# A hybrid decoder trunk: the point in the first layer at which the next layer's constants are loaded

## The chip, the cores and the metric

The kernel runs on one core of a Trainium2 chip. The metric is the device time of one execution in microseconds (us). The kernel before takes 841.26 us, the median of three runs (839.94 to 841.27). Engines are named as in the profile: PE (matmul), PEld (its weight loads), DVE (vector), ACT (scalar, activation functions), POOL, SP. "ACTq" and "SPq" are DMA issues of the ACT and the SP instruction stream.

## The reference

Two layers act on a stream of 256 tokens by 1024 channels. Each layer normalises the stream, projects it with one wide matrix, and feeds three mixers: a Mamba-2 scan (A), sliding-window attention (B) and forgetting attention (C). Their outputs are projected, weighted by gates, merged, projected once more and added to the stream. The lines that matter here:

```python
for layer in range(DEPTH):                       # DEPTH = 2
    h = rms_norm(x, norm_w[layer])
    proj = jnp.einsum('bsd,de->bse', h, w_in[layer])
    ... = jnp.split(proj, split_at, axis=-1)
    y_a = mamba2_branch(a_xbc, a_z, a_dt, conv_w[layer], conv_b[layer], dt_bias[layer],
                        a_log[layer], d_skip[layer], ssm_norm_w[layer])
    y_b = sliding_window_branch(b_q, b_k, b_v, b_z, sinks[layer], cos, sin)
    y_c = forgetting_attention_branch(c_q, c_k, c_v, c_f, c_z, f_bias[layer])
    branch = jnp.einsum('bsiw,iwd->bsid', jnp.stack([y_a, y_b, y_c], axis=2), w_proj[layer])
    g = jax.nn.sigmoid(gates.reshape(b, s, N_BRANCH, d) + gate_bias[layer])
    x = x + jnp.einsum('bsd,de->bse', jnp.sum(g * branch, axis=2), w_out[layer])
return rms_norm(x, final_norm_w)
```

The small parameters among these (`conv_w`, `conv_b`, `ssm_norm_w`, `norm_w`, `dt_bias`, `f_bias`, `sinks`, `a_log`, `d_skip`) are the "constants of a layer".

## The kernel before

**Matmuls.** Every dense product is made of three passes with operands split into a high and a low part: weights arrive from DRAM as 128x1024 float32 pieces (`raw`, six buffers, loaded by SP, line 345). ACT makes `hi` of a piece (L268), DVE makes `lo` = raw - hi (L269), and PE multiplies hi*hi, hi*lo and lo*hi (L97). When DVE has made `lo`, the `raw` buffer is free and SP issues the next load into it. So a late `hi` makes a late `lo`, and this makes a late load, six pieces further on.

**Order of the work.** The kernel writes a list of operations per layer (`op`): queries, keys and values of B, gates of B, the convolutions of A, then keys and queries of C (`u_ck`, `u_cq`, four pairs) with the gate path `z` of C among them, then `gates_proj(0)` (gates and projection of A) and `gates_proj(2)` (of C), then the output projection. Parts that hang on other engines (softmax, the scan) are generators that a "pump" enters between the matmuls. PE runs in the order in which this is written. The other engines are ordered by a scheduler at build time, except for instructions that are pinned to program order. The constants' loads are pinned (`pdma`).

**The constants.** `layer_consts` issues ten DMAs from ACT's instruction stream: `conv_w`, `conv_b` and `ssm_norm_w` into `vr`, `norm_w` into `nwb` (128x1024, broadcast to all partitions, 512 KB), `dt_bias`, `f_bias`, `sinks` and `a_log` into `hb`, and two halves of `d_skip` into `dsk`. POOL then scales `nwb` once. The profile names all of them L263, the line of the pinning helper. Nothing reads the second layer's constants before the end of the first layer. For the last layer the same place in the list holds `load_final`, which loads the weight of the final norm (L1085).

**DMA and semaphores.** Every DMA of SP and ACT counts up one of eight semaphores, DMAHW0 to DMAHW7, given out in rotation over both streams. Before an engine issues a DMA, its instruction stream waits until the DMA that had this semaphore before has landed. While ACT's stream waits so, the activations behind it in the stream wait too.

**Who waits for whom around the forgetting attention.** In the stretch that the change reaches, ACT evicts transposed probabilities from PSUM (L594), computes the `tanh` of a z path (L829) and makes `hi` (L268). DVE finishes z (L832), makes `lo` (L269), multiplies the scan's decays (L804, L805) and adds the scan's result (L815, tile `mx` to `L`). PSUM tiles `mx` rotate through five buffers, so that the last of four score tiles of the next attention quad (`mx<-qt`, L97) can be written only when the first L815 has read the buffer before.

Of the kernel before, what the change touches and what calls it, by code (L numbers as in the profile page):

```python
# [20 lines left out]
L = 2  # L21
# [23 lines left out]
def hybrid_trunk(  # L45
# [17 lines left out]
    def T(tag, shape, dtype=F32, bufs=None):  # L63
        count[0] += 1
        return sb.tile(shape, dtype, tag=tag, name=f"{tag}_{count[0]}",
                       bufs=bufs if bufs is not None else BUFS.get(tag, 1))
# [63 lines left out]
    def pump(budget=BUDGET):  # L130
        t0 = clock["t"]
        while clock["t"] - t0 < budget:
            for m in sorted(waiting, key=lambda m: (m[0], m[1])):
                if ready(m):
                    enter(m)
                    break
            else:
                return
# [119 lines left out]
    def halves(ap):  # L258

        return ap.rearrange("p (a i) -> p a i", a=2)  # L260

    def pin(f):
        return lambda *a, **k: tc.keep_in_program_order(f(*a, **k))  # L263
# [138 lines left out]
    layers = []  # L402
# [9 lines left out]
    def layer_consts(y):  # L412
        l = y.l
        vr = T("vr", [88, P])
        pdma(vr[0:64, :], conv_w[l].rearrange("j (u p) -> (j u) p", p=P))
        pdma(vr[64:80, :], conv_b[l:l + 1, :].rearrange("o (u p) -> (o u) p", p=P))
        pdma(vr[80:88, :], ssm_norm_w[l:l + 1, :].rearrange("o (u p) -> (o u) p", p=P))
        if l:
            y.nwb = T("nwb", [P, D])
            pdma(y.nwb, norm_w[l:l + 1, :].to_broadcast([P, D]))  # L420
            pin(nc.gpsimd.tensor_scalar)(y.nwb, y.nwb, -0.5, None, op0=ALU.mult)
        y.hb = T("hb", [P, 64], bufs=2)
        for i, v in enumerate((dt_bias, f_bias, sinks, a_log)):
            pdma(y.hb[:, 16 * i:16 * i + 16], v[l:l + 1, :].to_broadcast([P, 16]))
        y.dsk = T("dsk", [P, NK], bufs=2)
        for half in range(2):
            src = d_skip[l:l + 1, :].rearrange("o (j two) -> two o j", two=2)[half]
            pdma(y.dsk[64 * half:64 * half + 64, :], src.to_broadcast([64, NK]))
        y.vr = vr
# [14 lines left out]
    def chan(y, w, c):  # L444

        p = pmm()
        dense(p[:, 0:S], lambda k: w.hi(k)[:, c:c + P], lambda k: w.lo(k)[:, c:c + P],
              lambda k: tokens_in_turn(y.hTh, k), lambda k: tokens_in_turn(y.hTl, k), w)
        return ordered(p[:, 0:S])
# [433 lines left out]
    def u_ck(y, j, c):  # L883
        def f(w):
            p = chan(y, w, c)
            y.ckT[j] = T("qt", [P, 2, S])
            act(halves(y.ckT[j][:, 0, :]), p, AF.Copy)
            if j % 2 == 0:
                launch(2, fox_quad(y, j), D_FOX)
            pump()  # L890
        return f

    def u_cq(y, j, c):
        def f(w):
            p = chan(y, w, c)
            kq = y.ckT[j]
            act(halves(kq[:, 1, :]), p, AF.Copy)
            y.cqdone[j] = clock["t"]
            pump()
        return f  # L900
# [187 lines left out]
    def sub(src, n=256):  # L1088
        subs.append((src, n))
        return len(subs) - 1  # L1090

    def op(i, *fs):
        for f in fs:
            ops.append((i, f))

    for y in layers:
        l = y.l
# [3 lines left out]
        def cols(c0, n=256):  # L1101
            return sub([(0, w[:, c0:c0 + n])], n)

        def z1(c0, br, b):
            op(cols(c0 + 256 * b), u_z(y, br, 2 * b, 0), u_z(y, br, 2 * b + 1, P))
# [5 lines left out]
        def gates_proj(br):  # L1111
            def g(b):
                c = 512 * b
                op(cols(C_G + D * br + c, 512), u_gate(y, br, c, 0), u_gate(y, br, c, 1))

            def p(b):
                c = 512 * b
                if b == 0 and br != 0:
                    op(None, lambda y=y: split_late(y, br))
                i = sub([(0, w_proj[l, br, :, c:c + 512])], 512)  # L1120
                if b == 0 and br == 0:
                    op(i, u_proj2(y, br))
                else:
                    op(i, u_proj(y, br, c, 0), u_proj(y, br, c, 1))
            seq = [(g, 0), (p, 0), (g, 1), (p, 1)]
            if br == 0:
                seq = [(lambda b: z1(C_ZA, 0, b), b) for b in range(4)] + seq
            return [lambda f=f, b=b: f(b) for f, b in seq]
# [33 lines left out]
        for b, zb in enumerate(((), (0,), (1,), (2, 3))):  # L1162
            op(cols(C_CK + 256 * b), u_ck(y, 2 * b, 0), u_ck(y, 2 * b + 1, P))
            op(cols(C_CQ + 256 * b), u_cq(y, 2 * b, 0), u_cq(y, 2 * b + 1, P))
            for z in zb:
                z1(C_ZC, 2, z)
        for f in gates_proj(0):
            f()
        op(None, load_final if l + 1 == L else lambda: layer_consts(layers[1]))
        for f in gates_proj(2):  # L1170
            f()
        o = [sub([(0, w_out[l, :, c:c + n])], n) for c, n in ((0, 256), (256, 512), (768, 256))]
# [96 lines left out]
```

## Time and profile before

| what | value |
|---|---|
| median of three runs | 841.26 us (runs of 839.94, 841.26 and 841.27) |
| the profiled execution's own time | 840.8 us |
| its span | 839.1 us, so 1.7 us lie around the span |
| busy: PE, PEld, DVE, ACT, POOL | 824.1, 752.4, 642.5, 502.9, 130.3 us |
| mean granted PE clock | 0.997 |
| DMA | 158.41 MB, mean 189 GB/s |

The profile's page gives busy time by engine, the course of the span in 40 slices, the chain of work that ended last, and groups of instructions. The trace behind it gives each instruction's start, duration, the idle time ahead of it on its engine and what ended this idle time (in brackets, with an arrow). Times in rows are us from the start of the span.

### The profile page before, as it was taken

The numbers are of one execution on the slowest core, as the hardware profiler recorded it, in microseconds if no ns is written. First come the engines' busy times: TensorE is split into PE (matmuls) and PEld (weight loads), VectorE is DVE, ScalarE is ACT, GpSimd is POOL, SyncE is SP. The second block draws the span as 40 slices with busy tenths as digits, with TensorE's granted clock in tenths as the row PEclk, the third lists the DMA queues.
The fourth block names the chain that finished last, engine by engine and source line by source line (L and its number), as shares of the span: only waits on it lengthen the run. The fifth ranks groups of instructions, "written<-read, shape, count | busy, mean of one in ns | idle before, by whom it ended". The sixth has DMA issues, their size and how long they took to land.

```text
span 839.1 us, 15714 instructions
## 1 busy us (share of the span) xinstructions
PE 824.1 (98%) x5832; PEld 752.4 (90%) x5832; DVE 642.5 (77%) x1347; ACT 502.9 (60%) x978; POOL 130.3 (16%) x167
## 2 busy tenths in 40 slices
PE   7999999999999999999999999999999999999996
PEld 7989888989999998887989998898899999988896
DVE  5778987998766679647688889889968667785665
ACT  6466777665656667435555667775456667654442
POOL 7411300000231010210014122000003110121000
PEclk9999999999999999999999999999999999999999
DMA  8576565567475556647677465465756564476632
GB/s 303 164 231 199 178 201 164 176 214 226 140 210 173 157 165 205 206 167 266 205 230 225 151 201 177 144 189 199 240 168 187 161 186 155 150 238 213 214 102 74
DMA packets 123596, 158.41 MB, mean 189 GB/s; under 512 B 12784, under 2 KB 84192, under 8 KB 123520
## 3 DMA queue, kind: packets, MB, share of 16 engines
q1 hardware_dynamic: 109456, 140.79, 53.2%
q10 hardware_dynamic: 14016, 16.49, 6.5%
q8 instruction: 46, 0.75, 0.4%
q14 instruction: 30, 0.25, 0.1%
q0 software_dynamic: 48, 0.13, 0.0%
HBM read 155.22 MB, written 2.16 MB: 188 GB/s over the span
## 4 chain that ended last, share of the span: by engine, by line
PE 91%; DMA 5%; DVE 1%; issue 1%; ACT 1%; POOL 0%; SPq 0%; POOLq 0%; DVEq 0%; ACTq 0%
PE mm L97 79%; PE mx L97 9%; PE mx L101 4%; DMA raw<-in_w_in_dram 3%; DMA raw<-in_w_proj_dram 2%; DVE lo L269 0%; DMA hb<-in_sinks_dram 0%; ACT hi L268 0%; POOL lo L1201 0%; ACT hi L1200 0%; DVE L L474 0%; ACT L L1060 0%; DVE L L269 0%; DVE L L987 0%; DVE L L986 0%
## 5 line engine op out<-in xcount | busy, mean ns | idle before, releaser
L97 PE MATMUL mm<-hi,L 128*128 128x512 f32 (+1 forms) x1344 | 373.8, 364 | 1.9 <-ACT hi L1200 1.3
L269 DVE TENSOR_TENSOR lo<-raw,hi 128x1024 fp32r<-128x1024 f32 x252 | 307.8, 1236 | 88.1 <-ACT hi L268 80.8
L268 ACT ACTIVATE hi<-raw 128x1024 fp32r<-128x1024 f32 x252 | 262.8, 1055 | 94.6 <-PE mm L97 64.8
L97 PE MATMUL mm<-L,hi 128*128 128x256 f32 x1792 | 317.4, 278 | 0.8 <-DVE L L477 0.8
L97 PEld LDWEIGHTS mm<-L,hi 128*128 128x128 f32 x1792 | 277.7, 192 | 7.2 <-issue 3.9
L97 PEld LDWEIGHTS mm<-hi,L 128*128 128x128 f32 x1344 | 241.7, 190 | 32.3 <-issue 2.7
L97 PE MATMUL mm<-L,lo 128*128 128x256 f32 x896 | 246.6, 275 | 0.0
L97 PE MATMUL mm<-lo,L 128*128 128x512 f32 (+1 forms) x672 | 241.7, 361 | 0.1
L97 PEld LDWEIGHTS mm<-L,lo 128*128 128x128 f32 x896 | 172.0, 192 | 0.2
L97 PEld LDWEIGHTS mm<-lo,L 128*128 128x128 f32 x672 | 127.5, 190 | 14.8 <-POOL lo L1201 0.3
L914 POOL TENSOR_SCALAR_AFFINE_SELECT bias<-bias 128x128 f32<-128x128 f32 x64 | 39.8, 653 | 264.0 <-DVE L L793 173.0
L768 DVE SCALAR_TENSOR_TENSOR L<-L,vec,L 128x255 f32<-128x255 f32 (+2 forms) x96 | 46.8, 488 | 6.5 <-ACT L L765 5.1
L97 PE MATMUL mx<-L,L 128*64 128x128 f32 (+1 forms) x384 | 36.5, 332 | 0.0
L97 PEld LDWEIGHTS mx<-L,L 128*64 128x64 f32 x384 | 23.8, 137 | 11.7 <-issue 2.7
L640 ACT ACTIVATE pp<-pp,nm 128x128 f32<-128x128 f32 x64 | 25.1, 394 | 15.0 <-DVE nm L633 11.3
L565 ACT ACTIVATE pp<-pp,nm 128x128 f32<-128x128 f32 x64 | 28.2, 443 | 8.5 <-DVE nm L559 8.5
L938 ACT ACTIVATE L<-L 128x512 f32<-128x512 f32 x24 | 15.1, 629 | 28.6 <-DVE L L937 28.4
L829 ACT ACTIVATE L<-mm 128x256 f32<-128x256 f32 x48 | 18.1, 377 | 19.0 <-PE mm L97 18.9
L771 ACT ACTIVATE L<-L 128x256 f32<-128x256 f32 x32 | 13.3, 417 | 26.3 <-DVE L L768 25.7
L665 POOL TENSOR_SCALAR_AFFINE_SELECT L<-L 128x256 f32<-128x256 f32 x16 | 11.9, 743 | 109.2 <-ACT L L663 109.2
L101 PE MATMUL mx<-ident,L 128*128 128x128 f32 x144 | 22.3, 279 | 3.7 <-DVE L L987 2.1
L633 DVE CUSTOM_DVE_ANT_0 pp<-mx,wmask,nsink 128x128 f32<-128x128 f32 x64 | 24.2, 413 | 2.0 <-PE mx L97 1.8
(176 smaller groups left out, 756.7 us busy)
## 6 DMA issues: line engine op xcount, KB each, us to landing
raw<-in_w_in_dram SPq DMA_DIRECT2D x200, 512.0 KB, 4.6
raw<-in_w_proj_dram SPq DMA_DIRECT2D x48, 512.0 KB, 5.7
raw<-in_w_out_dram SPq DMA_DIRECT2D x16, 512.0 KB, 5.0
L<-cumd ACTq DMA_DIRECT2D x8, 512.0 KB, 4.5
bias<-cumd ACTq DMA_DIRECT2D x16, 256.0 KB, 3.8
L<-in_gate_bias_dram ACTq DMA_DIRECT2D x12, 256.0 KB, 4.0
L<-in_x_dram SPq DMA_DIRECT2D x2, 512.0 KB, 5.0
nwb<-in_norm_w_dram SPq DMA_DIRECT2D x1, 512.0 KB, 5.4
```

The lines of the kernel that those rows point to most:

```text
L97: nc.tensor.matmul(o, a, b, **kw)
L101: nc.tensor.transpose(o, a, i)
L268: keep(act)(hi, src, AF.Copy)
L269: keep(tt)(lo, src, hi.bitcast(F32), op=ALU.subtract)
L565: act(pp[:, i, sl], pp[:, i, sl], AF.Exp, scale=-1.0, bias=nm[:, e:e + 1], accum_out=sums[:, e:e + 1])
L633: nc.vector.tensor_tensor_reduce(out=pp[:, i, sl], in0=score(p, i, b), in1=m, scale=-0.125, scalar=ns[:, i:i + 1], op0=ALU.add, op1=ALU.mi ...
L640: act(pp[:, i, sl], pp[:, i, sl], AF.Exp, scale=-1.0, bias=nm[:, e:e + 1], accum_out=sums[:, e:e + 1])
L768: stt(a[:, s:S], x_[:, 0:S - s], y.vec[:, 16 * j + u:16 * j + u + 1], a[:, s:S], op0=ALU.mult, op1=ALU.add)
L771: act(th, a, AF.Tanh)
L829: act(halves(th), p, AF.Tanh, scale=0.5)
L914: nc.gpsimd.affine_select(out=bias[:, i, dst], in_=bias[:, i, src], compare_op=ALU.is_ge, fill=NEG, base=0, pattern=[[-1, P]], channel_mul ...
L938: act(g, g, AF.Tanh, scale=0.5)
```

## The change

One call moves up in the list of operations. In the first layer it is `layer_consts` of the second layer, in the second layer `load_final`. It stood between the projections of A and the gates of C, and now stands amid the keys and queries of C, behind the second of four pairs.

```diff
         for b, zb in enumerate(((), (0,), (1,), (2, 3))):
             op(cols(C_CK + 256 * b), u_ck(y, 2 * b, 0), u_ck(y, 2 * b + 1, P))
             op(cols(C_CQ + 256 * b), u_cq(y, 2 * b, 0), u_cq(y, 2 * b + 1, P))
+            if b == 1:
+                op(None, load_final if l + 1 == L else lambda: layer_consts(layers[1]))
             for z in zb:
                 z1(C_ZC, 2, z)
         for f in gates_proj(0):
             f()
-        op(None, load_final if l + 1 == L else lambda: layer_consts(layers[1]))
         for f in gates_proj(2):
             f()
```

PE's order of instructions is the same in both kernels, and SP's order of loads too. The load of the last norm's weight stays at its row in ACT's stream, early in the second layer, where the scheduler had put it already. What moves lies in the first layer.

**ACT, at the place that the loads leave** (gates of A and C; `hi` and `raw` are the weight pieces). Before:

```order
L268 ACTIVATE hi_4564<-raw_4465 128x1024
L263 DMA vr_4572<-in_conv_w_dram 64x128
L263 DMA vr_4572<-in_conv_b_dram 16x128
L263 DMA vr_4572<-in_ssm_norm_w_dram 8x128
L263 DMA nwb_4576<-in_norm_w_dram 128x1024
L263 DMA hb_4579<-in_dt_bias_dram 128x16
L263 DMA hb_4579<-in_f_bias_dram 128x16
L263 DMA hb_4579<-in_sinks_dram 128x16
L263 DMA hb_4579<-in_a_log_dram 128x16
L263 DMA dsk_4584<-in_d_skip_dram 64x8x1 x2
L268 ACTIVATE hi_4624<-raw_4477 128x1024
L268 ACTIVATE hi_4636<-raw_4489 128x1024
```

In the changed kernel the same stretch of ACT holds activations alone:

```order
L268 ACTIVATE hi_4488<-raw_4373 128x1024
L268 ACTIVATE hi_4500<-raw_4385 128x1024
L268 ACTIVATE hi_4543<-raw_4409 128x1024
L268 ACTIVATE hi_4555<-raw_4421 128x1024
L938 ACTIVATE L_854_4506<-L_854_4506 128x512
L268 ACTIVATE hi_4567<-raw_4468 128x1024
L268 ACTIVATE hi_4579<-raw_4480 128x1024
```

The ten issues are gone from between the second and the third `hi`, and the splits follow each other.

**ACT, at the place that the loads go to** (around the second quad of C; `L<-mx` at L594 are evictions of transposed probabilities, `L<-mm` at L829 the tanh of z). Before:

```order
L897 ACTIVATE qt_2777<-mm_2884 128x256
L798 ACTIVATE L_553_2863<-L_553_2863 128x1024
L268 ACTIVATE hi_3020<-raw_2731 128x1024
L897 ACTIVATE qt_2860<-mm_2910 128x256
L268 ACTIVATE hi_3038<-raw_2749 128x1024
L594 ACTIVATE L_566_2953<-mx_2948 128x512
L829 ACTIVATE L_572_2988<-mm_2962 128x256
L594 ACTIVATE L_574_2998<-mx_2955 128x512
L594 ACTIVATE L_576_3005<-mx_3000 128x512
L268 ACTIVATE hi_3177<-raw_2840 128x1024
L829 ACTIVATE L_584_3044<-mm_3007 128x256
```

Now, from the second `qt` on, with the semaphores for which each row waits (the three loads into `vr` stand ahead of this piece, one ahead of L798 and two behind it):

```order
L897 ACTIVATE qt_2860<-mm_2910 128x256 [waits PE_49]
L263 DMA nwb_2966<-in_norm_w_dram 128x1024 [waits DMAHW1_49]
L594 ACTIVATE L_566_2953<-mx_2948 128x512 [waits PE_49]
L263 DMA hb_2969<-in_dt_bias_dram 128x16 [waits DMAHW3_49]
L263 DMA hb_2969<-in_f_bias_dram 128x16 [waits DMAHW4_49]
L263 DMA hb_2969<-in_sinks_dram 128x16 [waits DMAHW5_49]
L263 DMA hb_2969<-in_a_log_dram 128x16 [waits DMAHW6_49]
L263 DMA dsk_2974<-in_d_skip_dram 64x8x1 [waits DMAHW7_49]
L263 DMA dsk_2974<-in_d_skip_dram 64x8x1 [waits DMAHW0_49]
L829 ACTIVATE L_576_3003<-mm_2977 128x256 [waits PE_49]
L594 ACTIVATE L_578_3013<-mx_2955 128x512 [waits PE_49]
L594 ACTIVATE L_580_3020<-mx_3015 128x512 [waits PE_49]
```

Seven issues now stand ahead of the tanh (L829). The two `hi` that stood ahead of the tanh (of raw_2731 and raw_2749) stand behind the two evictions, and the second tanh behind those. The wait of the `a_log` row is for the weight load raw_2927, which has DMAHW6 before it and which SP issues when DVE has made lo_2924.

**DVE, at the same place** (`lo` at L269, the scan's products at L804 and L805, z at L832, the scan's result at L815, then the scores' reductions at L559). Before:

```order
L269 TENSOR_TENSOR lo_2942<-raw_2648,hi_2941 128x1024
L269 TENSOR_TENSOR lo_3021<-raw_2731,hi_3020 128x1024
L269 TENSOR_TENSOR lo_3039<-raw_2749,hi_3038 128x1024
L832 SCALAR_TENSOR_TENSOR L_571_2987<-L_572_2988,mm_2962 128x256
L804 TENSOR_TENSOR L_553_2863<-L_553_2863,mx_2991 128x1024
L805 TENSOR_TENSOR L_556_2873<-L_556_2873,mx_2991 128x512
L269 TENSOR_TENSOR lo_3178<-raw_2840,hi_3177 128x1024
L832 SCALAR_TENSOR_TENSOR L_571_2987<-L_584_3044,mm_3007 128x256
L815 SCALAR_TENSOR_TENSOR L_364_1826<-L_364_1826,dsk_412,mx_3071 128x256
L815 SCALAR_TENSOR_TENSOR L_364_1826<-L_364_1826,dsk_412,mx_3077 128x256
L269 TENSOR_TENSOR lo_3196<-raw_2858,hi_3195 128x1024
L559 ISA pp_3083,nm_3085<-mx_3087,bias_2958 128x128
```

Now:

```order
L269 TENSOR_TENSOR lo_2942<-raw_2648,hi_2941 128x1024
L804 TENSOR_TENSOR L_553_2863<-L_553_2863,mx_3006 128x1024
L805 TENSOR_TENSOR L_556_2873<-L_556_2873,mx_3006 128x512
L832 SCALAR_TENSOR_TENSOR L_575_3002<-L_576_3003,mm_2977 128x256
L269 TENSOR_TENSOR lo_3036<-raw_2731,hi_3035 128x1024
L269 TENSOR_TENSOR lo_3054<-raw_2749,hi_3053 128x1024
L832 SCALAR_TENSOR_TENSOR L_575_3002<-L_588_3059,mm_3022 128x256
L815 SCALAR_TENSOR_TENSOR L_364_1826<-L_364_1826,dsk_412,mx_3086 128x256
L815 SCALAR_TENSOR_TENSOR L_364_1826<-L_364_1826,dsk_412,mx_3092 128x256
L559 ISA pp_3098,nm_3100<-mx_3102,bias_2958 128x128
```

The `lo` of raw_2731 and raw_2749 stand behind the first L832, so that L815 follows two splits and both L832, each of which waits for ACT. The `lo` of raw_2840 and raw_2858 have moved behind L559.

## The prediction

> **What bounds the kernel now.** I read the page first: the busy times, then the shares of the chain that ended last.
>
> ```profile
> PE 824.1 (98%) x5832; PEld 752.4 (90%) x5832; DVE 642.5 (77%) x1347; ACT 502.9 (60%) x978; POOL 130.3 (16%) x167
> PE 91%; DMA 5%; DVE 1%; issue 1%; ACT 1%; POOL 0%; SPq 0%; POOLq 0%; DVEq 0%; ACTq 0%
> ```
>
> PE bounds everything, and it is almost never idle. A change to loads can therefore only take away a gap of PE or make one, and a gap made anywhere goes straight into the end, since PE's order is fixed and full. So I looked for gaps. The two layers run the same code, and the only thing that the first does and the second doesn't, in this part, is loading the constants. The chain in order of time lets one lay the layers over each other: at the second attention quad, at the long run of gate matmuls, and behind it.
>
> ```profile
> 235.49 2.96 PE mx L97 x32
> ...
> 327.90 38.65 PE mm L97 x179
> ...
> 385.46 15.54 PE mm L97 x72
> ...
> 646.75 2.96 PE mx L97 x32
> ...
> 739.16 49.21 PE mm L97 x228
> ...
> 794.43 15.54 PE mm L97 x72
> ```
>
> The layers stand 411.26 us apart at the quad (646.75 - 235.49) and still at the start of the long run (739.16 - 327.90), but 408.97 behind it (794.43 - 385.46). The first layer thus loses 2.29 us between 327.9 and 385.5, which the second doesn't lose. PE's timeline has the gap in one row:
>
> ```profile
> 384.81 0.66 PE L101 MATMUL mx<-ident,L 128*128 128x128 f32 x4 [2.07 <-DVE L L987]
> ```
>
> PE waits 2.07 us for the merge on DVE (L987). Who made DVE late? ACT's timeline some 25 us earlier, and SP's load at its root:
>
> ```profile
> 356.26 0.34 ACTq L263 DMA_DIRECT2D hb<-in_f_bias_dram  x1
> 359.23 0.33 ACTq L263 DMA_DIRECT2D hb<-in_sinks_dram  x1
> 359.61 0.45 ACTq L263 DMA_DIRECT2D hb<-in_a_log_dram  x1
> 360.09 1.30 ACTq L263 DMA_DIRECT2D dsk<-in_d_skip_dram  x2
> 361.50 2.96 ACT L268 ACTIVATE hi<-raw 128x1024 fp32r<-128x1024 f32 x3 [6.76 <-DMA hb<-in_sinks_dram]
> ...
> 376.73 1.06 ACT L268 ACTIVATE hi<-raw 128x1024 fp32r<-128x1024 f32 x1 [6.51 <-DMA raw<-in_w_in_dram]
> ```
>
> ```profile
> 354.73 0.37 SPq L345 DMA_DIRECT2D raw<-in_w_in_dram  x1
> ```
>
> ```profile
> DMA to landing us min/median/max: 4.5/4.5/4.5
> ```
>
> Between the issues of `f_bias` and `sinks` ACT's stream stands still until 359.23. That is to the digit when the weight load of 354.73 has landed (354.73 + 4.5), the load that had the semaphore of `sinks` before it. With the issues ACT loses 6.76 us; its `hi` come late, so `lo`, so the buffers, so the next loads, for which ACT then waits 6.51 us at 376.73, and the merge behind them on DVE comes late for PE. The stall of the trace, then, is not the price of ten issues but that of a wait inside them.
>
> **What the change removes.** ACT's order at the old place becomes that of the second layer, row for row: no issue between the splits. The second layer has no gap there, so I take the whole difference of the layers: **-2.29 us**. What would be late next is nothing that the second layer shows. Bounds: nothing gained, if the gap had another cause, and 2.29.
>
> **What it adds.** The ten issues now stand amid the second quad. Their waits are given by the rotation of the semaphores. The one that ends last is that of `a_log`: it waits for the weight load that SP issues when DVE has finished the first of four `lo`:
>
> ```profile
> 227.28 4.72 DVE L269 TENSOR_TENSOR lo<-raw,hi 128x1024 fp32r<-128x1024 f32 x4
> ```
>
> ```profile
> 228.54 0.37 SPq L345 DMA_DIRECT2D raw<-in_w_in_dram  x1
> ```
>
> ```profile
> DMA to landing us min/median/max: 5.0/5.0/5.0
> ```
>
> Nothing ahead of that `lo` changes, so the load still goes out at 228.54 and lands at 233.54. From `a_log` to the next activation it took 1.89 us at the old place (361.50 - 359.61). So the tanh behind the issues (L829) starts at 235.43. Before the change it stood here:
>
> ```profile
> 231.54 0.38 ACT L829 ACTIVATE L<-mm 128x256 f32<-128x256 f32 x1 [0.42 <-PE mm L97]
> ```
>
> What is queued behind it on ACT is two evictions, two `hi`, the second tanh; and on DVE, in the new order, L832, two `lo`, L832, L815. A stretch with the same sequence of tanh, two evictions and `hi`, one quad later, gives ACT's steps, and the old order at this place DVE's:
>
> ```profile
> 277.81 0.39 ACT L829 ACTIVATE L<-mm 128x256 f32<-128x256 f32 x1 [0.23 <-PE mm L97]
> 278.09 1.08 ACT L594 ACTIVATE L<-mx 128x512 f32<-128x512 f32 x2
> 279.04 1.07 ACT L268 ACTIVATE hi<-raw 128x1024 fp32r<-128x1024 f32 x1
> ```
>
> ```profile
> 235.33 1.23 DVE L269 TENSOR_TENSOR lo<-raw,hi 128x1024 fp32r<-128x1024 f32 x1 [1.23 <-ACT hi L268]
> 236.47 0.42 DVE L832 SCALAR_TENSOR_TENSOR L<-L,mm 128x256 f32<-128x256 f32 x1
> 236.80 0.87 DVE L815 SCALAR_TENSOR_TENSOR L<-L,dsk,mx 128x256 f32<-128x256 f32 x2
> ```
>
> Step by step: `hi` starts 1.23 after the tanh (279.04 - 277.81), at 236.66, and ends 1.07 later, at 237.73. The first `lo` starts there; the second follows 1.16 later ((4.72 - 1.23) / 3 in the row of four), at 238.89; L832 follows 1.14 later (236.47 - 235.33), at 240.03, its own tanh having been done by then; L815 0.33 after that (236.80 - 236.47), at 240.36; and the first of the two L815 is done in half of 0.87, at 240.80. That one frees the PSUM buffer of the fourth score tile. PE comes to the second pair of score tiles, which holds it, here:
>
> ```profile
> 237.63 0.60 PE L97 MATMUL mx<-qt 64*128 64x128 f32 x5
> ```
>
> So PE waits from about 237.65 to 240.85: **+3.2 us**. The largest uncertainty is the landing, since the broadcast of `nwb` now shares the queues with it while two later weight loads leave. Its nearest rows are the shortest and the longest of this kind of load:
>
> ```profile
> L345 SPq DMA_DIRECT2D raw<-in_w_in_dram x1: 368/368/368, 236.6 to 236.6; - x1
> ...
> DMA to landing us min/median/max: 3.5/3.5/3.5
> ```
>
> ```profile
> L345 SPq DMA_DIRECT2D raw<-in_w_in_dram x1: 367/367/367, 25.3 to 25.3; - x1
> ...
> DMA to landing us min/median/max: 5.7/5.7/5.7
> ```
>
> 3.5 would make the gap 1.7, 5.7 would make it 3.9. I keep 5.0, the same load's own row.
>
> **What I cost at nothing.** The other lateness at the new place is that of the second quad's softmax. Its reductions on DVE follow L815 3.6 us later than before (240.36 against 236.80), less the one `lo` that no longer stands between (1.16), so 2.4; and two `lo` (1.16 each) now stand within the scaling, so this ends 4.7 later.
>
> ```profile
> 242.91 1.01 DVE L577 TENSOR_SCALAR pp<-pp,rsum 128x128 f32<-128x128 f32 x4
> ```
>
> ```profile
> 248.33 0.66 PE mx L101 x6
> ```
>
> PE transposes the first half of the probabilities at 248.33, 4.4 us after even the last scaling ends (243.92), and moves back by 3.2 itself; the cover is 7.6 against 4.7, and were it gone, each us over it would cost one. The next weight loads leave when the two `lo` are done, at about 239 and 240.1, and land 5 later, at 244 and 245.1; their splits stand in ACT's order behind the eviction of the transposes of 248.33. POOL's scaling of `nwb` falls into an idle stretch:
>
> ```profile
> 360.55 2.80 POOL L263 TENSOR_SCALAR nwb<-nwb 128x1024 f32<-128x1024 f32 x1 [2.01 <-DMA nwb<-in_norm_w_dram]
> ```
>
> ```profile
> 245.06 4.12 POOL L914 TENSOR_SCALAR_AFFINE_SELECT bias<-bias 128x128 f32<-128x128 f32 x8 [11.40 <-DMA bias<-cumd]
> ```
>
> Its 2.80 us lie in the 11.40 of idle time. The final norm's weight doesn't move in ACT's stream at all: 0.
>
> **The sum.** -2.29 + 3.2 = +0.9 us. The profiled execution took 840.8, so 841.7; the median of the runs stands 0.46 above that execution, so **842.2** against 841.26. With the landing's bounds: 840.7 to 842.9.
>
> **Rivals.** *The issues cost no wait (faster).* If `a_log` finds its semaphore free, the place decides the other way. The gap closes when the tanh starts 3.2 earlier, at 232.2, so with `a_log` issued by 230.3, 1.8 us after the weight load. No load of this kind is that quick (3.5 at best), so this needs the order of the semaphores to be read wrongly; the old place, where the wait matches to the digit, speaks against it. Price: the old gap goes, nothing comes, -2.29, so 839.0. The Trainium skill says in "DMA: Bandwidth & Descriptors", section "Issuing engines are not separate DMA queues", that the choice of issuing engine only matters for the time to initiate, "which is usually small relative to the DMA itself"; by that rule this rival would win. The stop of ACT's stream until 359.23 disagrees: what is paid on the issuer is a landing.
>
> *The clock falls in the new gap (slower).* Early in the program PE was starved, and its granted clock fell:
>
> ```profile
> 10.71 2.17 PE L97 MATMUL mm<-hi,L 128*128 128x256 f32 x8 [1.34 <-ACT hi L1200]
> ```
>
> ```profile
> 11.00:12.00 1.00, 0.98 (x5) 0.78 (x5) 0.97 (x4) 1.00 (x3) 0.75 (x1) 0.61 1.11 351
> ...
> 13.00:14.00 1.00, 1.00 (x6) 0.93 (x6) 0.58 (x1) 0.31 (x1) 1.00 (x2) 0.50 1.09 367
> ...
> 383.00:386.00 3.00, 1.19 (x8) 1.12 (x9) 2.95 (x5) 0.50 (x2) 0.00 (x0) 1.00 0.98 297
> ```
>
> Behind the five engines' busy times stand the clock, the DMA share and GB/s. The clock is 0.61, then 0.50: PE ran at half speed for some 3.3 us after several idle microseconds; after the gap of 2.07 at 384 it stayed at 1.00. A gap of 3.2 lies beyond what the trace shows to be harmless. If the clock falls for 3.3 us, half of that is lost, +1.7, so 842.2 + 1.7 = 843.9. It decides from a gap somewhere above 2.07. The Trainium skill puts it, in "TensorE: Matmul & The Clock Gate", section "Part 1: The HAM clock gate (the "warmup" mystery)", at one idle window of about 3.4 us; by that rule a gap of 3.2 is just spared and one of 3.9 may not be, and the trace agrees as far as 2.07 goes.
>
> *The old gap stays.* Then the change doesn't do what it says; +3.2 alone, 844.5. Against it speaks the second layer without the gap.
>
> **How the numbers follow.** The forecast's case (840.7 to 842.9) gets 0.55, no wait 0.13, the clock 0.17, the old gap staying 0.07, and 0.08 goes to lateness that I didn't find, mostly slower. The range leaves out the first and the last of the rivals (0.20): 839.9 to 844.1. About 0.2% (1.7 us) is what a measurement can tell from no change. Below 839.6 lies the no-wait rival: faster 0.14. Above 842.9 lie the clock, the staying gap and part of the rest: slower 0.29. Within: 0.57.
>
> **What would show it.** In the profile after: no idle time ahead of the merge's transposes near 384, and the layers there the same distance apart as at the long run's start; `a_log` issued at about 233.5 behind a stop of ACT's stream; L815 at about 240.4; an idle PE of some 3 us ahead of the score matmuls (`mx<-qt`), released by L815; the clock at 1.00 behind it. A landing far from 5 us, or a tanh at 232, would make the prediction wrong.

## The result, and the profile after

The changed kernel takes 842.32 us (median of 22 executions, 840.17 to 845.62), the kernel before 840.08 in as many on the same chip (838.25 to 842.45). The ratio is **1.0029** (95% interval 1.0020 to 1.0038): slower by 2.2 us, a little over the 0.2% that can be told from no change. The forecast time of 842.2 is hit almost exactly, but partly by luck. It stood on a median of 841.26 from three runs; 22 runs put that at 840.08. The forecast *difference* was +0.9, the measured one +2.2.

The profiled execution of the changed kernel took 840.68 us (span 839.0), that of before 840.8. So the profiled executions show hardly a difference where the medians do, and this turned out to be the question of the study. First the lines that answer to those of before. PE's waits and PE's timeline at the second quad of the changed kernel:

```profile
PE mx L97 <- DVE L L815: 1.6, 1, 1.6
```

```profile
236.89 1.14 PE L97 MATMUL mx<-qt 64*128 64x128 f32 x10
239.63 0.92 PE L97 MATMUL mx<-qt 64*128 64x128 f32 x6 [1.60 <-DVE L L815]
```

The wait for L987 near 384 is gone from the list, and a wait of 1.60 us for L815 is the longest. ACT, SP and the landing of SP's load, at that place:

```profile
229.84 0.45 ACTq L263 DMA_DIRECT2D hb<-in_f_bias_dram  x1
230.33 0.44 ACTq L263 DMA_DIRECT2D hb<-in_sinks_dram  x1
232.43 0.33 ACTq L263 DMA_DIRECT2D hb<-in_a_log_dram  x1
232.80 1.31 ACTq L263 DMA_DIRECT2D dsk<-in_d_skip_dram  x2
234.15 0.38 ACT L829 ACTIVATE L<-mm 128x256 f32<-128x256 f32 x1 [4.19 <-DMA hb<-in_f_bias_dram]
```

```profile
228.56 0.37 SPq L345 DMA_DIRECT2D raw<-in_w_in_dram  x1
```

```profile
DMA to landing us min/median/max: 3.9/3.9/3.9
```

ACT's stream stops between `sinks` (done at 230.77) and `a_log` (232.43), and 228.56 + 3.9 is 232.46: the wait is the predicted one, to within the rounding of the landing. The bracket behind L829 names the transfer of `f_bias`; the engine's idle time of 4.19 us is made up of the issues and of that stop, so the names of the rows in it tell more than the bracket. Behind the tanh, DVE:

```profile
234.57 0.42 DVE L832 SCALAR_TENSOR_TENSOR L<-L,mm 128x256 f32<-128x256 f32 x1 [0.47 <-ACT L L829]
236.49 2.36 DVE L269 TENSOR_TENSOR lo<-raw,hi 128x1024 fp32r<-128x1024 f32 x2 [1.50 <-ACT hi L268]
238.77 0.41 DVE L832 SCALAR_TENSOR_TENSOR L<-L,mm 128x256 f32<-128x256 f32 x1
239.10 0.87 DVE L815 SCALAR_TENSOR_TENSOR L<-L,dsk,mx 128x256 f32<-128x256 f32 x2
```

From tanh to L815 it is 4.95 us (239.10 - 234.15), where 4.93 was predicted. The two layers laid over each other, in the chain of the changed kernel (ahead of the quad, the long run, and behind it):

```profile
204.98 0.66 PE mx L97 x4
...
330.00 49.21 PE mm L97 x228
...
385.27 15.54 PE mm L97 x72
...
616.14 0.66 PE mx L97 x4
...
739.08 49.21 PE mm L97 x228
...
794.35 15.54 PE mm L97 x72
```

The layers stand 411.16 apart ahead of the quad, 409.08 at the long run and 409.08 behind it. The first layer now loses 2.08 us at the new place and nothing at the old one. The clock behind the gap (the numbers behind the five engines are clock, DMA share, GB/s):

```profile
238.00:240.00 2.00, 0.40 (x6) 0.37 (x6) 2.00 (x5) 1.57 (x2) 0.00 (x0) 1.00 0.05 0
240.00:242.00 2.00, 2.00 (x19) 1.67 (x16) 2.00 (x15) 1.79 (x9) 0.00 (x0) 1.00 0.05 0
```

It stays at 1.00. In this execution the sum is therefore -2.29 + 2.08 = -0.2, and the two profiled executions differ by -0.1.

The last two numbers of these rows, a DMA share of 0.05 and 0 GB/s, are worth a look too. From 236 to 244 us the DMA engines move next to nothing, and the weight loads issued at 237.74 and 238.88 land 10.7 and 12.1 us later, not the 5 of the prediction. The same stretch lies in the profile before, from 362 to 370:

```profile
364.00:368.00 4.00, 4.00 (x20) 3.52 (x19) 4.00 (x5) 3.92 (x5) 0.00 (x0) 1.00 0.05 0
```

Both times it follows the two issues of `d_skip` (232.80 and 360.09). In what comes below it is called the standstill. PE waits for none of the loads that it holds up in the changed kernel's traces, so it has no share in the 1.60 us above. For the old gap this is different, as the section on why the prediction was right says.

### The profile page after: what moved, and what is told of

Same layout as the page of the kernel before. It is cut to its first block, busy times and chain, and to the rows that moved or that the text cites. A ratio compares the mean times of both kernels' runs of the same rounds, so it can differ in the third digit from the quotient of the medians.

```text
span 839.0 us, 15709 instructions
## 1 busy us (share of the span) xinstructions
PE 824.3 (98%) x5832; PEld 752.2 (90%) x5832; DVE 642.9 (77%) x1347; ACT 503.5 (60%) x978; POOL 127.5 (15%) x167
## 4 chain that ended last, share of the span: by engine, by line
PE 90%; DMA 4%; ACT 2%; DVE 2%; issue 1%; POOL 0%; ACTq 0%; SPq 0%; POOLq 0%; DVEq 0%
PE mm L97 78%; PE mx L97 8%; DMA raw<-in_w_in_dram 4%; PE mx L101 3%; DVE lo L269 1%; DMA hb<-in_f_bias_dram 1%; ACT hi L268 0%; ACT hi L1201 0%; ACT pp L565 0%; POOL L L1221 0%; ACTq L263 0%; ACT L L268 0%; DVE L L796 0%; DVE L L793 0%; DVE pp L577 0%
## 5 line engine op out<-in xcount | busy, mean ns | idle before, releaser
L269 DVE TENSOR_TENSOR lo<-raw,hi 128x1024 fp32r<-128x1024 f32 x252 | 308.1, 1236 | 80.0 <-ACT hi L268 70.9
L914 POOL TENSOR_SCALAR_AFFINE_SELECT bias<-bias 128x128 f32<-128x128 f32 x64 | 37.3, 615 | 264.5 <-DMA bias<-cumd 177.6
L829 ACT ACTIVATE L<-mm 128x256 f32<-128x256 f32 x48 | 18.2, 378 | 22.5 <-PE mm L97 18.2
L937 DVE TENSOR_TENSOR L<-mm,L 128x512 f32<-128x512 f32 x24 | 16.5, 687 | 14.7 <-PE mm L97 14.7
```

The lines of the kernel that those rows point to most:

```text
L269: keep(tt)(lo, src, hi.bitcast(F32), op=ALU.subtract)
L829: act(halves(th), p, AF.Tanh, scale=0.5)
L914: nc.gpsimd.affine_select(out=bias[:, i, dst], in_=bias[:, i, src], compare_op=ALU.is_ge, fill=NEG, base=0, pattern=[[-1, P]], channel_mul ...
L937: tt(halves(g), p, halves(y.gb), op=ALU.add)
```

## The experiments

"Ratio" is always to the kernel before, run beside it on the same chip, with its 95% interval in brackets.

### Both kernels again, a filled gap, and the issues on POOL

The kernel before, again:

> The kernel before, unchanged, beside itself: its ratio should be 1.000. It is run for the granted clock of its executions. Theory 'clock' (a gap of PE of about 1.6 to 3 us, at the second attention quad, lets PE's clock fall in a part of the executions): the median clock of the kernel before lies above that of the changed kernel, whose 22 executions have a median of 0.995, so at 0.997 or more, though it has a gap of 2.07 us of its own. Rival 'length' (the changed kernel is slower only because the weight load lands later in most executions than the 3.9 us of the profiled one, so the gap is longer): the clocks of both kernels are the same, 0.995.

Measured: 840.01, ratio 0.9995 (0.9984 to 1.0006), clock 0.9975 (median). In its profiled execution PE waits 1.4 us for L987, where it was 2.07 before: the old gap varies too.

The changed kernel, again:

> The changed kernel once more, on the same chip as the others: a ratio near 1.003 again, and a second profiled execution. Theory 'length': the gap ahead of the score matmuls is longer here or the time is again that of a fast execution; the gap follows the landing of the weight load, 5.42 + 1.89 us behind it less what lies ahead. Theory 'clock': executions with the lower mean clock are the longer ones, about 0.8 us for each 0.001.

Measured: 843.7 (841.74 to 845.47), ratio 1.0032 (1.0017 to 1.0047), clock 0.995 (median). Its profiled execution took 841.76, near the lowest of its 12, with a wait for L815 of 1.9 us and the clock at 1.00 behind it.

The gap filled with 28 passes (a new argument of the quad's function, `fill`, is 14 for the second quad of the first layer's forgetting attention and 0 elsewhere; each of these float32 matmuls shows as two passes in the trace):

```diff
+                    if fill and p == 1 and b == 0 and i == 0:
+                        for _ in range(fill):
+                            nc.tensor.matmul(score(1, 0, 0), qTs[1][0:64, 0:P], kTs[1][0:64, 0:P],
+                                             start=True, stop=True)
                     mm(score(p, i, b), qTs[p][r, b * P:(b + 1) * P], kTs[p][r, 0:(b + 1) * P],
                        start=True, stop=True)
```

> The changed kernel with 14 small matmuls (about 1.5 us of PE work in all) written into the third score tile of the second quad, ahead of that tile's own score, which overwrites them. They stand where PE waits, so the gap of 1.60 us becomes PE work. Theory 'clock': the clock no longer falls after the gap, the median clock rises to that of the kernel before, and the time falls by 1 to 1.7 us against the changed kernel, to a ratio near 1.001 against the kernel before. Rival 'length': PE waits for the same moment, so the time is that of the changed kernel, ratio near 1.003, and the clocks stay at 0.995.

Measured: 841.93 (840.62 to 843.03), ratio 1.0013 (1.0003 to 1.0022). PE at the place, and the landing of the load for which `a_log` waits (the added lines make L815 into L819):

```profile
238.02 3.28 PE L552 MATMUL mx<-qt 64*128 64x128 f32 x28
241.15 0.38 PE L97 MATMUL mx<-qt 64*128 64x128 f32 x2
241.70 0.49 PE L97 MATMUL mx<-qt 64*128 64x128 f32 x3 [0.17 <-DVE L L819]
```

```profile
DMA to landing us min/median/max: 5.5/5.5/5.5
```

The fill took 3.28 us, twice what I had estimated, and the landing was 5.5 here, so that even 3.28 us of work did not reach L815 (0.17 idle). Yet the kernel is faster than the changed kernel beside it by 1.8 us.

All ten issues of the second layer's constants on POOL, at the new place:

```diff
-    pdma = pin(nc.scalar.dma_start)
+    pdma_act, pdma_next = pin(nc.scalar.dma_start), pin(nc.gpsimd.dma_start)

     def layer_consts(y):
         l = y.l
+        pdma = pdma_next if l else pdma_act
```

> The changed kernel with the second layer's constants issued by POOL instead of ACT, at the same place of the list. ACT's stream has no issue and no wait in it then. My theory (the stop of ACT's stream, which waits for a weight load's landing, makes both the old gap and the new one): both gaps are gone and nothing comes, -2.3 us against the kernel before, ratio near 0.997. Rival 'transfers' (it is the transfers themselves, 512 KB of broadcast and many small packets, that delay the weight loads): a gap at the new place stays, ratio near 1.000 or above.

Measured: 838.6 (837.73 to 839.94), ratio **0.9976** (0.9965 to 0.9987). Neither gap is there, and the executions lie within 2.2 us of each other. This version beats both kernels. It changes more than the issuer, though: "the new place" is one of the list of operations only. In the trace POOL, which is ahead of the others there, issues the ten loads at 95 to 108 us, so the `d_skip` loads (107.21) and their standstill are far from both gaps.

What I concluded then, too early: the issues' waits are the whole effect. The rest of the difference seemed to be the clock, since the changed kernel's executions had a median clock of 0.995, the filled and the POOL kernel 0.997. The next runs were made for that.

### Which place, which issue, how much fill

The issues on POOL at the *old* place (the same edit on the kernel before):

> The kernel before with one edit: the second layer's ten constants are issued from POOL's instruction stream instead of ACT's, at the old place in the list. Theory (an issue of ACT that waits for the landing of a weight load is the whole cost, the place as such costs nothing): PE's wait at 384 for the merge at L987 is gone, layers as far apart there as ahead of it, and the time falls as it did with POOL at the new place, ratio 0.9976 (0.9965 to 0.999). Rival (the 512 KB that travel beside the weight loads at the old place make the gap, whoever issues them): the gap of 1.4 to 2.1 us stays and the ratio is 1.000.

Measured: 838.62 (837.92 to 839.68), ratio 0.998 (0.9971 to 0.999). PE's wait for L987 is gone, and the time falls as the theory said. The 512 KB beside the weight loads make no gap: POOL issues `norm_w` at 361.35, between weight loads. But `d_skip` goes out at 372.05 here instead of 360.09, and the loads that land late behind it (13.2 to 13.4 us for those issued at 375 to 378) are other ones than before, which PE doesn't wait for. So the run shows that the ten issues on ACT make the old gap; whether by ACT's stop or by the `d_skip` transfers at that moment it does not tell apart.

Only `a_log` and the two halves of `d_skip` on POOL, the other seven issues on ACT at the new place:

```diff
+    pdma, ppool = pin(nc.scalar.dma_start), pin(nc.gpsimd.dma_start)
...
-            pdma(y.hb[:, 16 * i:16 * i + 16], v[l:l + 1, :].to_broadcast([P, 16]))
+            (ppool if l and i == 3 else pdma)(y.hb[:, 16 * i:16 * i + 16], v[l:l + 1, :].to_broadcast([P, 16]))
...
-            pdma(y.dsk[64 * half:64 * half + 64, :], src.to_broadcast([64, NK]))
+            (ppool if l else pdma)(y.dsk[64 * half:64 * half + 64, :], src.to_broadcast([64, NK]))
```

> The changed kernel with only the last three of the ten issues (a_log and the two halves of d_skip) moved to POOL's stream; the other seven, the 512 KB of norm_w among them, stay on ACT at the new place. Theory (one wait, that of a_log's issue for the weight load that has its semaphore, makes the gap): the tanh at L829 starts at about 230.8 instead of 234 to 235, L815 about 5 us later at 236, before PE needs it at 238, so the gap is gone and the ratio is 0.9965 to 0.999, as with all ten on POOL. Rival (the issues' own time on ACT, some 4 us, or the 512 KB beside the weight loads makes it): a wait of 1 us or more for L815 stays, ratio 1.000 or more.

Measured: 839.38 (838.43 to 840.09), ratio 0.9989 (0.998 to 0.9998). ACT and DVE:

```profile
230.00 0.48 ACTq L263 DMA_DIRECT2D hb<-in_f_bias_dram  x1
230.52 0.44 ACTq L263 DMA_DIRECT2D hb<-in_sinks_dram  x1
231.81 0.38 ACT L829 ACTIVATE L<-mm 128x256 f32<-128x256 f32 x1 [2.30 <-PE mm L97]
```

```profile
236.89 0.87 DVE L815 SCALAR_TENSOR_TENSOR L<-L,dsk,mx 128x256 f32<-128x256 f32 x2
```

With seven issues ahead of it the tanh now waits for its matmul (bracket: PE), not for a load, L815 starts at 236.89, and PE waits for it nowhere. Here POOL issues `a_log` at 235.40 and `d_skip` at 236.06, so the standstill is at the new place (1 GB/s from 240 to 243, landings of 13.8 to 14.1 us for the weight loads issued at 236.67 to 242.39), and still PE has no gap: the standstill alone doesn't make the new one. ACT loses two things with the three issues, the stop of `a_log` (1.66 us, 230.77 to 232.43 in the changed kernel) and their own 1.6 us. An estimate from the changed kernel's rows puts it on the stop: without it the tanh would start at 232.49, and the first L815 would be done at 237.9, just before PE stops at 238.03. The ratio is 0.0013 above that of the kernel with all ten on POOL, 1.1 us; the two intervals overlap, and it stays unexplained.

The changed kernel with 6 instead of 14 matmuls in the gap (`fill=6`):

> The changed kernel with 6 small matmuls (12 passes of 0.117 us, 1.4 us in all, by the 3.28 us that 28 passes took) in the first layer's second attention quad, put into the third score tile ahead of its own score. They need nothing that is late, so PE works on for 1.4 us where it stood, and the gap's length is set by the late L815 as before. The output is the reference's. Theory (the gap costs its length and, in most executions, a fall of the clock behind it): with 0.2 to 2 us of idle time left the clock stays at 0.997 on the mean, and the time is that of the gap's length alone, ratio to before 1.0000 to 1.0013 (the larger fill gave 1.0013 with 3.45 us of work and idle time). Rival (no clock in it: the landing is just later in most executions than in the two profiled ones): the fill changes nothing, ratio 1.0032 and clock 0.995.

Measured: 842.61 (839.71 to 843.94), ratio 1.0026 (1.0015 to 1.0036), clock 0.997 (median). **Here my theory of the clock failed.** The clock was back, as it said; the time was not, as the rival said. And in this set of runs the kernel before itself had a median clock of 0.995 (0.9975 in the set above) at an unchanged 840.41 us. So a mean clock that differs by 0.002 between sets of runs is no measure of lost time. The traces show a reason: in five of the fourteen the clock falls between 10 and 20 us, long ahead of the quad (the rows at 11 and 13 us in the prediction are one of them). The run of 24 matmuls ahead of the quad starts at 188.33 to 189.59 us in these five and at 187.61 to 189.13 in the other nine, so this fall hardly costs time, but it lowers the mean.

The changed kernel once more, for its trace:

> The changed kernel once more, for its trace. Theory (the clock falls behind the gap in most executions): if this execution's mean granted clock is 0.995 or less, the trace shows PE's clock below 1.00 somewhere in the 10 us behind the wait for L815 at about 238 to 241; if it is 0.997 or more, no fall there, and a gap of at most 2 us. Rival (landing only): a gap of 3 us or more, landing of the waited load 5 us or more, and the clock 1.00 behind it.

Measured: 840.3, clock 0.996. PE's row in this execution:

```profile
239.35 0.92 PE L97 MATMUL mx<-qt 64*128 64x128 f32 x6 [1.71 <-DVE L L815]
```

A short wait again, clock 1.00 behind it (the low mean comes from 13 to 16 us, at 0.50): it decides nothing, since the execution was again one of the quickest.

### A gap of fixed length

To part the gap's length from the landing, the next kernels have the issues on POOL (no gap, 838.6) and hold L815 up by one instruction on DVE:

```diff
+            if (y.l, g, j) == (0, 3, 0):
+                nc.vector.tensor_reduce(T("dum", [P, 8]), bc(py[:, 0:S], 1, 8), mybir.AxisListType.X, ALU.add)
             stt(y.xs[:, u, :], y.xs[:, u, :], y.dsk[:, u:u + 1], py[:, 0:S], op0=ALU.mult, op1=ALU.add)
```

> No wait of ACT here: the kernel is the one with all ten constants on POOL at the new place (ratio 0.9976, no gap), and one instruction is added on DVE, just ahead of the first layer's L815 in question: a sum over the same PSUM tile, read 8 times (128x2048 elements, an estimated 2.3 us, thrown away). So PE stands for L815 at the same place as in the changed kernel, for a fixed 1.2 to 1.6 us and without a DMA in it. Theory (a gap at this place costs its length, and what makes the changed kernel slower than its profiled executions is a landing that is later in most others): 838.6 + 1.2 to 1.6, so ratio 0.999 to 1.0000, executions spread over about 2 us as without a gap. Rival (the clock falls behind a gap of this size): another 1.2 to 1.8 us on top, ratio 1.001 to 1.002, and a mean clock 0.001 to 0.002 below that of the kernel without a gap.

Measured: 841.13 (839.84 to 843.2), ratio 1.0005 (0.9991 to 1.0019), clock 0.996 (median). DVE and PE (L815 is L818 here):

```profile
236.62 2.28 DVE L817 TENSOR_REDUCE dum<-mx 128x8 f32<-128x2048 f32 x1
238.82 0.86 DVE L818 SCALAR_TENSOR_TENSOR L<-L,dsk,mx 128x256 f32<-128x256 f32 x2
```

```profile
239.44 0.89 PE L97 MATMUL mx<-qt 64*128 64x128 f32 x6 [1.61 <-DVE L L818]
```

PE's wait is that of the changed kernel's profiled execution, 1.61 against 1.60, made without a wait for a transfer. The ratio fell between the two theories, and the executions spread over 3.4 us, not over the 2 of the theory.

With 16 readings (`[P, 16]`, `bc(..., 1, 16)`):

> As the run with 8 readings, with 16 (128x4096 elements, an estimated 4.4 us), so that PE stands for a fixed 3.3 to 3.8 us at that place. Theory (a gap costs its length): 838.6 + 3.3 to 3.8, ratio 1.0015 to 1.0025, spread about 2 us. Rival (the clock falls behind the gap): ratio 1.003 to 1.0045, and the trace shows PE below 1.00 within 10 us behind the gap.

Measured: 844.9 (844.4 to 846.18), ratio 1.0055 (1.0043 to 1.0068). PE, and the clock by windows:

```profile
241.54 1.22 PE L97 MATMUL mx<-qt 64*128 64x128 f32 x6 [3.74 <-DVE L L818]
242.69 0.58 PE L97 MATMUL mm<-L,hi 128*128 128x256 f32 x1
...
248.28 0.38 PE L97 MATMUL mm<-L,hi 128*128 128x256 f32 x1
```

```profile
241.50:242.50 1.00, 0.96 (x6) 0.53 (x6) 1.00 (x8) 0.47 (x3) 0.00 (x0) 0.73 0.00 0
242.50:243.50 1.00, 1.00 (x5) 0.81 (x5) 1.00 (x9) 1.00 (x6) 0.00 (x0) 0.50 0.00 0
243.50:244.50 1.00, 1.00 (x6) 1.00 (x6) 1.00 (x6) 1.00 (x5) 0.00 (x0) 0.50 0.00 0
244.50:246.00 1.50, 1.50 (x12) 1.50 (x11) 1.50 (x5) 1.15 (x6) 0.00 (x0) 0.71 0.00 0
246.00:248.00 2.00, 2.00 (x23) 1.59 (x23) 1.23 (x6) 0.38 (x1) 0.00 (x0) 1.00 0.81 201
```

Here the clock does fall: 0.73, 0.50, 0.50, 0.71, then 1.00 (the first number behind the engines), which loses 0.27 + 0.50 + 0.50 + 1.5 x 0.29 = 1.7 us, and the same matmul takes 0.58 instead of 0.38. The rival held, and the ratio is above even its 1.0045: 844.9 is 6.3 above 838.6 for a wait of 3.74. The Trainium skill ("TensorE: Matmul & The Clock Gate", section "Part 1: The HAM clock gate (the "warmup" mystery)") puts the fall at an idle window of about 3.4 us; the two lengths tried agree, with 1.61 spared and 3.74 not. But the fall early in the profile before came behind two shorter waits, 1.64 and 1.34 us, with 1.32 us of work between them, so the length of one wait is not the whole rule.

The changed kernel a fourth time, for its trace:

> The changed kernel once more, for its trace. Theory (the time follows the landing of the weight load that the a_log issue waits for): the execution's time is 839.0 plus the length of PE's wait for L815, to within 1 us; with an execution of 843 us or more the landing is 6 us or later. Rival (the clock): such an execution shows a short wait and a clock below 1.00 behind it.

Measured: 839.48, and a wait of 1.61:

```profile
238.54 0.92 PE L97 MATMUL mx<-qt 64*128 64x128 f32 x6 [1.61 <-DVE L L815]
```

The rule, 839.0 plus the wait, misses by 1.1, and once more no late execution was caught.

The fixed wait of 1.61 with the 6 matmuls in it:

> The fixed wait of the run with 8 readings (1.61 us, no DMA in it) filled with 6 small matmuls (12 passes, 1.4 us), the same that were put into the changed kernel, where the time was 842.6 and 4.0 above the kernel without a gap. Theory (a fixed gap costs its length, what came on top was the clock, and the rest of the changed kernel's time is a landing that is later in most executions): 838.6 + 1.6 = 840.2, ratio 0.9985 to 1.0000, executions within about 2 us. Rival one (the clock is not it): 841.1 and a spread of 3.4 us as with the bare wait, ratio 1.0005 or more. Rival two (the fill itself costs time, which would explain 842.6 without a late landing): 842 or more, ratio 1.002.

Measured: 840.77 (839.65 to 842.54), ratio 1.0000 (0.9989 to 1.0012), clock 0.998. It does not tell rival one from the theory, but rival two falls: the same fill stands in the changed kernel at 1.0026 (1.0015 to 1.0036), and these intervals don't meet. The fill is not what costs. (The executions spread over 2.9 us.)

### What the runs give together

One view measures the place alone: in each profiled execution's chain, the way from a run of 24 matmuls ahead of the quad to the long run of gates. Before (whose 327.90 is shown above), then POOL at the new place, the changed kernel and the fixed wait of 3.74:

```profile
188.70 5.38 PE mm L97 x24
```

```profile
188.49 5.38 PE mm L97 x24
...
327.70 49.21 PE mm L97 x228
...
382.97 15.54 PE mm L97 x72
```

```profile
188.72 5.38 PE mm L97 x24
...
330.00 49.21 PE mm L97 x228
```

```profile
188.48 5.38 PE mm L97 x24
...
333.48 49.21 PE mm L97 x228
```

| kernel | PE's wait at the quad (us) | way (us) | profile: above no gap | medians: above no gap |
|---|---|---|---|---|
| issues on POOL, new place | none | 139.21 | 0 | 0 |
| issues on POOL, old place | none | 139.21 | 0 | 0.3 |
| three issues on POOL | none | 139.20 | 0 | 1.1 |
| fixed wait, 8 readings | 1.61 | 141.27 | 2.06 | 2.4 |
| the same with 12 passes in it | 1.50 of work, 0.27 idle | 141.26 | 2.05 | 2.0 |
| fixed wait, 16 readings | 3.74 | 145.00 | 5.79 | 6.6 |
| changed kernel (four profiled executions) | 1.60, 1.9, 1.71, 1.61 | 141.28 to 141.60 | 2.07 to 2.39 | 4.5 and 4.7 |
| the same with 12 passes in the gap | 1.50 of work, 0.38 idle | 141.41 | 2.20 | 4.2 |
| the same with 28 passes in the gap | 3.28 of work, 0.17 idle | 142.98 | 3.77 | 3.1 |

The way of before is 139.20 (327.90 - 188.70). The last column is (ratio - 0.9976) x 840.3 us, since the sets ran on different chips; with the intervals of the ratios it is good to about 1 us.

A wait of 1.6 us costs 2.07: some 0.47 more than PE's idle time is lost around it. For the three kernels whose wait is of fixed length, the medians cost what the profiled execution shows, to within 0.8 us. For the changed kernel they cost some 2 us more, with and without 12 passes in the gap. Two things are special there: the wait goes back to a transfer's landing, and the standstill follows it. With 28 passes in it the kernel is back at what its trace shows.

## Why the prediction was right, and where not

**The old gap: its size right, its cause half shown.** "-2.29": before, the way from 327.90 to 385.46 is 57.56; on POOL it is 55.27 (382.97 - 327.70), and so it is after the change (385.27 - 330.00). The difference is 2.29. In medians the removal alone is worth 1.7 to 2.0 us (ratios 0.998 and 0.9976). The prediction put the gap down to "a wait inside" the ten issues, which makes `hi`, `lo` and the next loads late. The wait of 6.51 us at 376.73 is more than that: it ends with the landing of a weight load that went out at 363.84 and took 12.8 us, in the standstill, where 4.5 was the load's time at 354.73. The chain of the profile before passes through such a landing too:

```profile
366.71 13.29 DMA raw<-in_w_proj_dram
```

ACT's stop makes these loads late, and the standstill holds them up once more. No run takes away one and leaves the other at that place, so their shares stay open.

**The new wait, its place and its chain: right.** `a_log` waits for the landing of the weight load issued at 228.54 (228.56 after), tanh, evictions, two `hi`, two `lo`, L815 follow as worked out, and taking `a_log` and the two `d_skip` issues off ACT removes the gap. What was costed at nothing cost nothing in the profiled executions: no other wait appears, and from the long run on the layers keep their distance. One of its grounds was wrong, however: the next two weight loads do not land "at 244 and 245.1" but at 248.40 and 251.00, in the standstill, which the prediction doesn't have.

**The size of the new wait: wrong.** The step that failed is "So PE waits from about 237.65 to 240.85: +3.2 us", with its bounds of 1.7 to 3.9. Its largest term was misread. The landing of 5.0, called the same load's own row, comes from a view of two loads:

```profile
L345 SPq DMA_DIRECT2D raw<-in_w_in_dram x2: 368/368/368, 228.5 to 229.7; - x2
...
DMA to landing us min/median/max: 5.0/5.0/5.0
```

Taken one by one, the 5.0 is that of the load of 229.7; for the load of 228.54 the trace before has no landing. Nor are 3.5 and 5.7 the shortest and the longest of their kind: over the whole trace before these loads take 3.2 to 14.2 us. So the landing was a guess, and its bounds were too narrow. In the profiled execution it was less: the landing took 3.9, not 5.0, the tanh came 1.72 after `a_log`, not 1.89, PE stopped at 238.03, and 2.08 us were lost. In most executions it was more. The medians give 1.0029 / 0.9976 = 1.0053, that is +4.5 us (843.7 - 838.6 = 5.1 where both ran on one chip), above the upper bound of 3.9, though not clearly, since with the intervals of both ratios it is 3.3 to 5.6. That a shorter wait was profiled hides it: with 2.08 the change would be a tie, as the profiled executions of both kernels are (840.8 and 840.64 before; 840.68, 841.76, 840.30 and 839.48 after).

**Why it is more in most executions is not shown.** Holding L815 up by a fixed amount, with the same 1.61 in the profile, gives 1.0005 (0.9991 to 1.0019) and not 1.0029 (1.0020 to 1.0038), and with 12 passes in the gap it is 1.0000 against 1.0026, intervals apart again. So the excess comes with the issues on ACT or with their transfers, not with a gap of that length. Three explanations are left.

- *A later landing.* The load for which `a_log` waits goes out 0.3 us behind the start of ACT's issue of `norm_w` (512 KB), and the traces show two courses. In five, that issue is drawn out to 1.1 to 1.4 us, the weight load lands first, after 3.9 to 4.2 us, and `norm_w` after 5.5 to 5.8. In the kernel with 28 passes and that with three issues on POOL it takes 0.36 us, `norm_w` lands first, after 4.1 to 4.2, and the weight load after 5.4 to 5.5. The changed kernel's profiled execution, then the one with 28 passes:

```profile
228.23 1.08 ACTq L263 DMA_DIRECT2D nwb<-in_norm_w_dram  x1
```

```profile
228.60 0.36 ACTq L263 DMA_DIRECT2D nwb<-in_norm_w_dram  x1
```

  With the second course the changed kernel's wait would be 1.60 + 1.6 = 3.2 and its cost about 3.7, an estimate from these rows, not far from the 4.5 of the medians. All five traces with the first course are of quick executions (4th of 22, 2nd of 12, 1st of 12, and two single ones of 840.30 and 839.48); the kept execution is the first in the list of its set each time, so it need not be a typical one. The trace with 28 passes is of the second longest of its 12 (842.65). So this is the likeliest explanation.
- *The clock.* With a wait near 3.7 us it would fall as in the run with 16 readings. The kernel with 28 passes, where PE hardly stands idle, is lowest of the three (1.0013, 1.0003 to 1.0022), as this would have it, but its interval meets that of the kernel with 12 passes (1.0015 to 1.0036).
- *The standstill.* Behind it weight loads land 10 to 12 us after their issue. PE waits for none of them in the traces, and the kernel with three issues on POOL has it as well at 0.9989; with everything later in a slow execution it could still cost something.

No execution above 842 of the changed kernel was caught in a trace, so how often the second course comes, and with it the cause of the excess, stays open.

**The rivals.** "The issues cost no wait" is refuted. The Trainium skill ("DMA: Bandwidth & Descriptors", section "Issuing engines are not separate DMA queues") has it that issuing from several engines saves only the time to initiate, which is usually small. Here that time holds a wait for another load's landing, and moving the ten issues from ACT to POOL, with the change of their times that it brings, is worth 0.24%. "The clock falls in the new gap" named a real mechanism, half speed after 3.74 us of idle time and 1.7 us lost, the price that the prediction gave; behind the new gap it is absent in the changed kernel's four traces. "The old gap stays" is refuted.

## What to carry to other kernels

An instruction stream that issues a DMA can stop for another engine's load, the one that had the semaphore before; put small loads on a stream that nothing on the critical path shares, here POOL, where both places in the list that were tried did equally well. Then look in the trace when they really go out, and at the DMA rate behind them: behind two loads of 2 KB all the others stood still here. Where a wait ends with a landing, a kept trace is one execution and perhaps a quick one: bound the term by the landings of single loads over the whole trace, and compare many executions before calling two versions equal.

## What the runs showed of the hardware that was not expected

- After a wait of 3.74 us PE ran at 0.50 of its clock and was back at 1.00 by 246.0, 4.5 us behind the gap's end: 5.79 us lost for 3.74 idle.
- 64x128 float32 matmuls issued back to back took 0.117 us a pass (3.28 us for 28), twice my estimate. As a filler they take the wait's time but keep PE at work.
- The 128x4096 sum on DVE over a broadcast PSUM tile took 4.42 us, the 128x2048 one 2.28, close to the estimates of 4.4 and 2.3.
- Behind each pair of `d_skip` loads (2 KB each) the DMA engines moved about 1 GB/s or less for some 8 us: 362 to 370 before, 236 to 244 after, 376 to 384 with the issues on POOL at the old place. Weight loads issued in or just ahead of these stretches took 10 to 14 us to land; many others take 3.4 to 5.5. No run leaves out the `d_skip` loads, so that they are the cause is inferred from the order alone.
- Sets of executions of the same kernel differed in median clock by 0.002 (0.9975 and 0.995) without a difference in time.
